# The seven products of a block step, in one fixed order

## The chip, the cores and the metric

The kernel runs on one core of one Trainium2 chip. The time is the device's own, in microseconds, from one execution of the whole program; a figure for a kernel is the median of several runs. The core has five engines that work side by side, each through its own list of instructions in order: TensorE (PE in the profile; its weight loads, which overlap the matmuls, are PEld), VectorE (DVE), ScalarE (ACT), GpSimd (POOL) and SyncE (SP), which here only starts transfers from the main memory. TensorE writes its sums to PSUM, a small memory of banks; ScalarE and VectorE read them there.

## The reference

Two layers of a diffusion backbone over 512 tokens of 1024 channels. The first mixes tokens by attention, the second by a Fourier transform; each ends in a gated feed-forward network (FFN) with a width-3 convolution over the tokens, between RMS norms that a conditioning vector scales and shifts:

```python
def conv_ffn(h, w_up, conv_w, conv_b, w_down):
    u = h @ w_up
    up = jnp.pad(u, ((0, 0), (1, 1), (0, 0)))
    u = up[:, :-2] * conv_w[0] + up[:, 1:-1] * conv_w[1] + up[:, 2:] * conv_w[2] + conv_b
    gate, val = jnp.split(u, 2, axis=-1)
    return (jax.nn.silu(gate) * val) @ w_down
```

Here `h` is 512 x 1024, `w_up` 1024 x 5632 and `w_down` 2816 x 1024. All is float32, and the result is the token stream after both layers.

## The kernel before

Everything is kept transposed: channels on the 128 partitions, tokens along the free axis. A float32 product is made of three matmuls on a rounded format (float32r): each operand is split into a high part, the rounded value, and a low part, what is left over, and `mm3` (lines 107 to 110) issues weight high x moving high (L108), weight high x moving low (L109) and weight low x moving high (L110) into the same PSUM tile. In the profile's rows the moving operand stands first, the weight second, so `mm<-hl,wh` is L109 and `mm<-hh,wl` is L110. `split` (L131) makes the parts: ScalarE casts the high one, VectorE subtracts to get the low one.

The hidden width of the FFN, 2816, is 22 steps of 128 columns; each makes one tile of the gate and one of the value (both 128 x 512), convolves them (L1412 on ScalarE, L1413 and L1415 on VectorE), gates them (L1425, L1426) and splits the result for the down product, which follows in groups of steps. Most steps, 10 in the first layer's FFN and 14 in the second's, are *block steps*. There the product of the two weight blocks (each 8 slices of 128 rows) with `h` is done as a 2 x 2 block product with seven block multiplications in place of eight: the weight is a 2 x 2 array (gate or value, first or second half of the channels), and so is `h` (halves of the channels, halves of the tokens). `seven_inputs` (L1296) forms the sums of blocks of `h` once for an FFN; products 1, 2 and 3 use blocks of `h` itself (`hh`, `hl` in the rows), products 4 to 7 the sums (`zh`, `zl`). `seven_weights` (L1310) forms the sums of weight blocks for each step, with three operations of VectorE (L1315, L1317, L1318), and splits them in four pieces: the weight of product 1; of 5 and 7; of 6 and 3; of 2 and 4. High and low parts of weights (`wh`, `wl`) go through five tiles each; the raw weights that arrive by DMA, and the sums, share three tiles (`raw`). A cast that finds no free weight tile waits until TensorE has read one for the last time.

`seven_products` (L1329) multiplies. Each product is 4 slices x 3 = 12 matmuls of 128 x 128 x 256. Two PSUM tiles of one bank each take them, x (which becomes the gate) and y (the value), each with a left and a right half of 256 columns:

| product | goes to | what reads it |
|---|---|---|
| 1 | right of y | copy L1349 into `xs`, left |
| 5 | right of x | copy L1351 into `ys`, right |
| 2 | left of x | |
| 6 | right of y, on top of 1 | copy L1354 into `xs`, right |
| 4 | left of y | |
| 3 | right of x, on top of 5 | add L1357: x + `xs` |
| 7 | right of y, on top of 6 | copy L1359 into `ys`, left; add L1360: y + `ys` |

The copies run on ScalarE, the adds on VectorE. TensorE may not write to a tile while a copy reads from it, whichever half either touches.

The list of each engine is not the order of the source. A planner orders all instructions before the program runs, by their place in the source, by what depends on what, and by its own estimate of times; an instruction that its estimate holds up is passed by one that is ready. `follow(i, j)` (L113) ties instruction i behind j on the same engine, without a semaphore. Before the change, it ties the first matmul of a product behind the last of the product that opened its tile (1 for y, 5 for x) and leaves the rest to the planner.

Of the kernel before, what the change touches and what calls it, by code (L numbers as in the profile page):

```python
# [85 lines left out]
def kernel(ctx: ExitStack, tc: tile.TileContext, a):  # L86
# [5 lines left out]
    def mk(pool, shape, dt=F32, tag=None, bufs=1):  # L92
        cnt[0] += 1
        n = nbufs.setdefault((id(pool), tag), (pool, bufs))[1]
        return pool.tile(shape, dt, tag=tag, name=f"{tag}_{cnt[0]}", bufs=n)
# [11 lines left out]
    def mm3(out, ah, al, bh, bl, start, stop, skip=False):  # L107
        i = PE.matmul(out, lhsT=ah, rhs=bh, start=start, stop=False, skip_group_check=skip)  # L108
        PE.matmul(out, lhsT=ah, rhs=bl, start=False, stop=False, skip_group_check=skip)  # L109
        return i, PE.matmul(out, lhsT=al, rhs=bh, start=False, stop=stop, skip_group_check=skip)  # L110


    def follow(i, j):  # L113
        tc.add_manual_dep(i.ins, j.ins.name, mybir.DependencyInfo(
            mybir.DependencyClass.NoSync, mybir.DependencyReason.DATA), reason="order")
# [553 lines left out]
    with ExitStack() as es:  # L669
# [27 lines left out]
        with ExitStack() as e1:  # L697
# [305 lines left out]
            for g, kind in enumerate(["kb", "vb", "qa"]):  # L1003
# [5 lines left out]
                for sh, sl, t0, kb in (blocks if kind[0] != "q" else blocks[:2]):  # L1009
                    ps = mk(pps, [P, 2, 256], F32, "mm", 6)  # L1010
# [26 lines left out]
        with ExitStack() as e2:  # L1037
# [86 lines left out]
            for head in range(8):  # L1124
# [6 lines left out]
                for j in range(TT):  # L1131
                    qs = slice(j * P, (j + 1) * P)
                    ps = S0.pop() if S0 else mk(aps, [P, 1024], F32, "S", 2)
# [176 lines left out]
    def seven_weights(l, fi):  # L1310
        r = raw([P, 2, KC, P], a["w_up"][l, fi])
        s = mk(wp, [P, 4, KH, P], F32, "raw", 3)
        a4 = r.rearrange("p i (c k) n -> p (i c) k n", c=2)

        for j in (V.tensor_tensor(out=s[:, 0:2], in0=a4[:, 3::-3], in1=a4[:, 2].unsqueeze(1).to_broadcast(  # L1315
                      [P, 2, KH, P]), op=ALU.add),
                  V.tensor_tensor(out=s[:, 2], in0=s[:, 0], in1=a4[:, 0], op=ALU.add),  # L1317
                  V.tensor_tensor(out=s[:, 3], in0=s[:, 2], in1=a4[:, 1], op=ALU.add)):  # L1318
            held(j)
        w = {}  # L1320
        for names, src in (("1", a4[:, 0:1]), ("57", s[:, 0:2]), ("63", s[:, 2:4]), ("24", a4[:, 1::2])):
            wh, wl = wpair([P, len(names), KH, P])
            split(wh, wl, src)
            for i, n in enumerate(names):
                w[n] = wh[:, i], wl[:, i]
        return w


    def seven_products(l, fi, pps, bs):  # L1329
        w = seven_weights(l, fi)  # L1330
        x, y = (mk(pps, [P, T], F32, "mm", 6) for _ in range(2))
        xs, ys = (mk(cp, [P, T], F32, "sq", 2) for _ in range(2))
        begun = {}


        def product(n, ps, h):
            (wh, wl), (bh, bl) = w[n], bs[n]
            new = id(ps) not in begun
            m = []
            for k in range(KH):  # L1340
                m += mm3(ps[:, halves[h]], wh[:, k, :], wl[:, k, :], bh[:, k, :], bl[:, k, :], new and k == 0,
                         k == KH - 1, True)
            if new:
                begun[id(ps)] = m[-1]
            else:
                follow(m[0], begun[id(ps)])

        product("1", y, 1)
        S.copy(out=xs[:, :HT], in_=y[:, HT:])  # L1349
        product("5", x, 1)  # L1350
        S.copy(out=ys[:, HT:], in_=x[:, HT:])  # L1351
        product("2", x, 0)
        product("6", y, 1)
        S.copy(out=xs[:, HT:], in_=y[:, HT:])  # L1354
        product("4", y, 0)
        product("3", x, 1)
        V.tensor_tensor(out=x, in0=x, in1=xs, op=ALU.add)  # L1357
        product("7", y, 1)
        S.copy(out=ys[:, :HT], in_=y[:, HT:])  # L1359
        V.tensor_tensor(out=y, in0=y, in1=ys, op=ALU.add)  # L1360
        return x, y
# [27 lines left out]
    def ffn(l, xp, ready, pre, mid, gem, plain=None):  # L1389
# [168 lines left out]
        for gi, (f0, nch) in enumerate(GROUPS[l]):  # L1558
            end = gi == len(GROUPS[l]) - 1
            for fi in range(max(f0, FIRST), f0 + nch):  # L1560
                if fi == SUMS[l]:
                    bs = seven_inputs(xp)
                if fi in SEVEN[l]:
                    cc = [conv(fi, i, u, None, i == 1) for i, u in enumerate(seven_products(l, fi, pps, bs))]
                else:
                    cc = []
                    for i, w in enumerate(up_weights(l, wpair, [fi])):
                        ps = mk(pps, [P, T], F32, "mm", 6)
                        m = [up_mm(ps, w, s) for s in halves]
                        follow(m[1][0][0], m[0][-1][1])  # L1570
                        cc.append(conv(fi, i, ps))
                gated(fi, cc[0], cc[1], f0)
                if l == 0 and fi not in SEVEN[l] and fi > FIRST + 4:
                    pump(gem, GP[0])
                if l:
                    pump(down, DOWN.get(fi, 0))
# [365 lines left out]
```

## Time and profile before

| | us |
|---|---|
| median of three runs | 1110.64 (1109.5 to 1110.91) |
| the profiled execution, its own time | 1112.16 |
| its span, first to last instruction | 1110.4 |
| PE busy | 1081.1 (97%) |
| VectorE busy | 894.8 (81%) |
| ScalarE busy | 595.2 (54%) |
| GpSimd busy | 128.5 (12%) |
| granted TensorE clock, mean | 0.996 of full |

The profile gives start and duration of each instruction, and for an engine's idle time what ended it. Matmuls overlap in the engine's pipeline: one lasts 0.28 us, but in an undisturbed run the next starts 0.11 us after it. So a TensorE that is shown busy may still be late, and the distance between starts is read instead. The 24 block steps lie between 357 and 607 us (first layer) and between 831 and 1055 us (second layer) of the span.

### The profile page before, as it was taken

What the parts mean: (1) busy time and instruction counts of PE and PEld (TensorE: products, weight loads), DVE (VectorE), ACT (ScalarE), POOL (GpSimd) and SP (SyncE); (2) the same over time, 40 slices, a digit from 0 to 9 for tenths busy, and PEclk for the clock granted to TensorE, in tenths of its full rate; (3) what the DMA queues carried; (4) which work ended last, traced back from release to release, by engine and by line L of the source; (5) the groups of instructions that cost most, each with busy time, mean ns of one, the idle gap of its engine ahead of it and who ended that gap; (6) DMA issues with size and microseconds to landing.
All of it is one profiled execution on the core that took longest, in us unless ns stands there. A gap on an engine that the chain in (4) does not pass through costs nothing.

```text
span 1110.4 us, 22277 instructions
## 1 busy us (share of the span) xinstructions
PE 1081.1 (97%) x9220; PEld 1011.4 (91%) x9220; DVE 894.8 (81%) x1459; ACT 595.2 (54%) x1048; POOL 128.5 (12%) x136
## 2 busy tenths in 40 slices
PE   9999999999999999999999998999999999999995
PEld 5699888869999999999999997989999999999995
DVE  5778877763689967878999788878997998979756
ACT  4442356665665633552556446668755654655543
POOL 0046123412100000000000133300000000000012
PEclk9999999999999999999999999999999999999998
DMA  9675100273231565227624600923205433332342
GB/s 368 273 256 209 39 7 33 76 275 143 77 153 43 181 233 213 106 86 272 236 77 175 231 22 21 279 82 143 86 29 198 145 107 118 105 103 88 106 148 77
DMA packets 33774, 156.01 MB, mean 140 GB/s; under 512 B 3460, under 2 KB 8196, under 8 KB 22024
## 3 DMA queue, kind: packets, MB, share of 16 engines
q1 hardware_dynamic: 32520, 150.39, 37.6%
q0 software_dynamic: 1152, 4.19, 1.5%
q8 instruction: 72, 1.18, 0.4%
q14 instruction: 30, 0.25, 0.1%
HBM read 148.28 MB, written 6.29 MB: 139 GB/s over the span
## 4 chain that ended last, share of the span: by engine, by line
PE 69%; DVE 18%; ACT 6%; DMA 4%; issue 2%; POOL 1%; SPq 0%; DVEq 0%; POOLq 0%; ACTq 0%
PE mm L108 20%; PE mm L109 18%; PE mm L110 18%; DVE wl L131 4%; ACT wh L131 2%; PE PT L1081 1%; DVE cv L1413 1%; DVE cv L1415 1%; DMA raw<-in_w_up 1%; DVE md_t L330 1%; DVE xT L332 1%; PE gm L108 1%; ACT yT L352 1%; PE O L109 1%; PE gm L110 1%
## 5 line engine op out<-in xcount | busy, mean ns | idle before, releaser
L131 ACT CAST wh<-raw 128x1024 fp32r<-128x1024 f32 (+2 forms) x207 | 190.7, 932 | 147.3 <-PE mm L109 96.9
L131 DVE TENSOR_TENSOR wl<-raw,wh 128x1024 fp32r<-128x1024 f32 (+2 forms) x205 | 219.4, 1076 | 59.3 <-ACT wh L131 56.7
L108 PE MATMUL mm<-hh,wh 128*128 128x256 f32 x856 | 240.2, 282 | 2.5 <-ACT sq L1351 1.8
L110 PE MATMUL mm<-hh,wl 128*128 128x256 f32 x856 | 236.9, 277 | 1.7 <-DVE wl L131 1.7
L109 PE MATMUL mm<-hl,wh 128*128 128x256 f32 x856 | 237.0, 277 | 0.4 <-DVE hl L355 0.3
L108 PEld LDWEIGHTS mm<-hh,wh 128*128 128x128 f32 x856 | 160.4, 188 | 8.5 <-ACT sq L1351 6.1
L110 PEld LDWEIGHTS mm<-hh,wl 128*128 128x128 f32 x856 | 160.9, 188 | 2.2 <-DVE wl L131 2.1
L109 PEld LDWEIGHTS mm<-hl,wh 128*128 128x128 f32 x856 | 160.8, 188 | 0.8 <-DVE hl L355 0.5
L108 PE MATMUL mm<-xh,wh 128*128 128x256 f32 x492 | 136.8, 279 | 0.0
L109 PE MATMUL mm<-xl,wh 128*128 128x256 f32 x492 | 136.6, 278 | 0.0
L110 PE MATMUL mm<-xh,wl 128*128 128x256 f32 x492 | 136.4, 277 | 0.0
L108 PE MATMUL mm<-zh,wh 128*128 128x256 f32 x384 | 109.4, 285 | 0.7 <-ACT sq L1354 0.5
L109 PE MATMUL mm<-zl,wh 128*128 128x256 f32 x384 | 106.3, 277 | 0.0
L110 PE MATMUL mm<-zh,wl 128*128 128x256 f32 x384 | 106.2, 277 | 0.0
L108 PEld LDWEIGHTS mm<-xh,wh 128*128 128x128 f32 x492 | 92.4, 188 | 1.2 <-issue 0.8
L109 PEld LDWEIGHTS mm<-xl,wh 128*128 128x128 f32 x492 | 92.4, 188 | 0.6 <-issue 0.4
L110 PEld LDWEIGHTS mm<-xh,wl 128*128 128x128 f32 x492 | 92.5, 188 | 0.1
L108 PEld LDWEIGHTS mm<-zh,wh 128*128 128x128 f32 x384 | 72.1, 188 | 6.0 <-ACT sq L1354 5.4
L110 PEld LDWEIGHTS mm<-zh,wl 128*128 128x128 f32 x384 | 72.2, 188 | 0.0
L109 PEld LDWEIGHTS mm<-zl,wh 128*128 128x128 f32 x384 | 72.1, 188 | 0.0
L305 POOL TENSOR_TENSOR gacc<-gacc,sq 128x256 f32<-128x256 f32 (+1 forms) x23 | 20.2, 880 | 396.8 <-ACT sq L303 396.4
L1412 ACT ACTIVATE cv<-mm,cols 128x512 f32<-128x512 f32 x59 | 45.8, 778 | 10.8 <-PE mm L110 6.1
(457 smaller groups left out, 2795.7 us busy)
## 6 DMA issues: line engine op xcount, KB each, us to landing
raw<-in_w_up SPq DMA_DIRECT2D x42, 1024.0 KB, 4.9
xT<-in_mod_r SPq DMA_DIRECT2D x20, 1024.0 KB, 5.0
raw<-in_w_down SPq DMA_DIRECT2D x32, 384.0 KB, 3.1
raw<-in_mod_p SPq DMA_DIRECT2D x8, 1024.0 KB, 5.0
raw<-in_w_down SPq DMA_DIRECT2D x16, 512.0 KB, 4.3
raw<-in_w_in SPq DMA_DIRECT2D x6, 1024.0 KB, 8.2
yT<-in_mod_r SPq DMA_DIRECT2D x10, 512.0 KB, 6.6
raw<-in_w_out SPq DMA_DIRECT2D x4, 1024.0 KB, 5.9
```

The source lines that it names most:

```text
L108: i = PE.matmul(out, lhsT=ah, rhs=bh, start=start, stop=False, skip_group_check=skip)
L109: PE.matmul(out, lhsT=ah, rhs=bl, start=False, stop=False, skip_group_check=skip)
L110: return i, PE.matmul(out, lhsT=al, rhs=bh, start=False, stop=stop, skip_group_check=skip)
L131: i = S.copy(out=h, in_=src), eng.tensor_tensor(out=l, in0=src, in1=f(h), op=ALU.subtract)
L305: G.tensor_tensor(out=self.acc[:, sl], in0=self.acc[:, sl], in1=sq[:, sl], op=ALU.add)
L330: m = V.scalar_tensor_tensor(out=t, in0=yT[:, k, hs], scalar=der[:, l, gi, k:k + 1], in1=R, op0=ALU.mult, op1=ALU.mult)
L332: return m, (eng or (G if k % 2 else V)).tensor_tensor(out=xT[:, k, hs], in0=xT[:, k, hs], in1=t, op=ALU.add)
L352: S.activation(out=yT[:, c, halves[h]], in_=yT[:, c, halves[h]], func=AF.Identity, bias=bm[:, c:c + 1], scale=am[:, c:c + 1])
L1081: PE.transpose(out=pt[:, j * P:(j + 1) * P], in_=Ps[j][:, off:off + P], identity=ident)
L1412: S.activation(out=cv, in_=ps, func=AF.Identity, bias=bc, scale=wc[1])
L1413: V.scalar_tensor_tensor(out=cv[:, 1:], in0=ps[:, :T - 1], scalar=wc[0], in1=cv[:, 1:], op0=ALU.mult, op1=ALU.add)
L1415: V.scalar_tensor_tensor(out=cv[:, :T - 1], in0=ps[:, 1:], scalar=wc[2], in1=cv[:, :T - 1], op0=ALU.mult, op1=ALU.add)
```

## The change

The products are issued in the order 1, 5, 6, 2, 3, 4, 7 instead of 1, 5, 2, 6, 4, 3, 7, and the first matmul of each is tied behind the last matmul of the product in front of it in that order, whichever tile it goes to. Copies and adds keep their places behind the products that they read. The first matmul that clears a tile's bank stays the first of 1 and of 5. Nothing else is different; the block steps of both FFNs go through this function.

```diff
         w = seven_weights(l, fi)
         x, y = (mk(pps, [P, T], F32, "mm", 6) for _ in range(2))
         xs, ys = (mk(cp, [P, T], F32, "sq", 2) for _ in range(2))
-        begun = {}
-
+        begun, last = {}, []
 
         def product(n, ps, h):
             (wh, wl), (bh, bl) = w[n], bs[n]
@@
             for k in range(KH):
                 m += mm3(ps[:, halves[h]], wh[:, k, :], wl[:, k, :], bh[:, k, :], bl[:, k, :], new and k == 0,
                          k == KH - 1, True)
-            if new:
-                begun[id(ps)] = m[-1]
-            else:
-                follow(m[0], begun[id(ps)])
+            begun[id(ps)] = True
+            if last:
+                follow(m[0], last.pop())
+            last.append(m[-1])
 
         product("1", y, 1)
         S.copy(out=xs[:, :HT], in_=y[:, HT:])
         product("5", x, 1)
         S.copy(out=ys[:, HT:], in_=x[:, HT:])
-        product("2", x, 0)
         product("6", y, 1)
         S.copy(out=xs[:, HT:], in_=y[:, HT:])
-        product("4", y, 0)
+        product("2", x, 0)
         product("3", x, 1)
         V.tensor_tensor(out=x, in0=x, in1=xs, op=ALU.add)
+        product("4", y, 0)
         product("7", y, 1)
         S.copy(out=ys[:, :HT], in_=y[:, HT:])
         V.tensor_tensor(out=y, in0=y, in1=ys, op=ALU.add)
```

## The prediction

> **What bounds the kernel now.** I read the page first, for the engine that is never free and for the chain that ended last.
>
> ```profile
> span 1110.4 us, 22277 instructions
> PE 1081.1 (97%) x9220; PEld 1011.4 (91%) x9220; DVE 894.8 (81%) x1459; ACT 595.2 (54%) x1048; POOL 128.5 (12%) x136
> ...
> PE 69%; DVE 18%; ACT 6%; DMA 4%; issue 2%; POOL 1%; SPq 0%; DVEq 0%; POOLq 0%; ACTq 0%
> ```
>
> TensorE carries the program, VectorE is next, and 69% of the last chain is matmuls. Second, I cut the 24 block steps out of the span: one window each, from the first matmul of product 1 to the first matmul behind product 7. The columns are length, then busy time and count of PE, PEld, DVE, ACT and POOL, then clock and DMA. Five of the 24 rows, and the sum over all:
>
> ```profile
> 356.83:367.60 10.77, 10.21 (x87) 9.82 (x85) 10.77 (x14) 6.76 (x11) 0.00 (x0) 1.00 0.30 99
> ...
> 543.19:553.45 10.26, 10.09 (x86) 9.70 (x85) 10.22 (x14) 7.05 (x12) 0.00 (x0) 1.00 0.53 194
> ...
> 596.56:606.93 10.37, 10.20 (x88) 9.80 (x86) 10.37 (x14) 6.85 (x11) 0.00 (x0) 1.00 0.58 206
> ...
> 886.93:898.41 11.48, 10.37 (x87) 9.78 (x85) 11.04 (x15) 6.33 (x10) 0.00 (x0) 1.00 0.37 127
> ...
> 1012.16:1022.27 10.11, 10.09 (x87) 9.70 (x85) 9.70 (x15) 5.65 (x10) 0.00 (x0) 1.00 0.44 148
> ...
> sum 247.61, PE 243.66 PEld 234.32 DVE 202.89 ACT 136.94 POOL 0.00; mean PE 10.15 PEld 9.76 DVE 8.45 ACT 5.71 POOL 0.00
> ```
>
> Every window holds 84 matmuls (7 products x 4 slices x 3), and PE looks busy in nearly all of it. The starts of single matmuls say something else. Here is PE in the window at 1012, around the two places that matter (start, duration, line, operands; zh marks products 4 to 7, hh products 1 to 3):
>
> ```profile
> 1014.77 0.28 PE L110 MATMUL mm<-zh,wl 128*128 128x256 f32 x1
> 1014.88 0.28 PE L108 MATMUL mm<-zh,wh 128*128 128x256 f32 x1
> ...
> 1015.22 0.28 PE L108 MATMUL mm<-zh,wh 128*128 128x256 f32 x1
> 1015.50 0.39 PE L108 MATMUL mm<-hh,wh 128*128 128x256 f32 x1
> 1015.73 0.28 PE L109 MATMUL mm<-hl,wh 128*128 128x256 f32 x1
> ...
> 1018.23 0.28 PE L108 MATMUL mm<-hh,wh 128*128 128x256 f32 x1
> 1018.52 0.39 PE L108 MATMUL mm<-zh,wh 128*128 128x256 f32 x1
> 1018.74 0.28 PE L109 MATMUL mm<-zl,wh 128*128 128x256 f32 x1
> ```
>
> Three matmuls take 1015.22 - 1014.88 = 0.34 us, 0.1133 from start to start; 0.28 is only the length of one in the pipeline. The order on PE is not the source's: product 5 (to 1014.77), four matmuls of 6, product 2 (1015.50), the other eight of 6, four of 3 (the last at 1018.23), product 4 (1018.52), the rest of 3, product 7. Ahead of 2 and ahead of 4 the spacing is 0.28 and then 0.23 instead of 0.11. The release rows name the cause:
>
> ```profile
> 1015.08 0.37 ACT L1351 COPY sq<-mm 128x256 f32<-128x256 f32 x1 [0.37 <-PE mm L110]
> ...
> 1018.09 0.37 ACT L1354 COPY sq<-mm 128x256 f32<-128x256 f32 x1 [1.07 <-PE mm L110]
> ```
>
> Call the copies behind products 1, 5 and 6 A, B and C (L1349, L1351, L1354). B ends at 1015.45 and product 2, which writes the other half of the tile B reads, starts at 1015.50; C ends at 1018.46 and product 4 starts at 1018.52. From the last matmul of a product to the first that may follow its copy pass 1015.50 - 1014.77 = 0.73 us, and only four matmuls (0.45 us) stand in between.
>
> **The change part by part.** Nothing is added or taken from the arithmetic: 84 matmuls, four copies and two adds a block stay. What changes is the order: 1, 5, 6, 2, 3, 4, 7, none cut open.
>
> *What is removed.* 24 x 84 = 2016 matmuls at 0.1133 are 228.4 us; the windows sum to 247.61, so 19.2 us are stall. The plain block at 1012 has 10.11 - 9.52 = 0.59, of which the two waits make (0.28 + 0.23 - 0.23) + (0.29 + 0.22 - 0.23) = 0.56. In the new order 12 matmuls (1.36 us) stand between 5 and 2, and 24 (2.72 us) between 6 and 4, against the 0.73 us needed: both waits go. With 12 in between the next start is due 13 x 0.1133 = 1.47 us after the last, with 24 it is 2.83, so a copy may be 0.74 and 2.1 us late before PE feels it.
>
> *What is late next.* Some stall stays.
>
> ```profile
> 891.87 0.38 PE L110 MATMUL mm<-hh,wl 128*128 128x256 f32 x1 [1.04 <-DVE wl L131]
> ...
> 567.72 0.28 PE L110 MATMUL mm<-zh,wl 128*128 128x256 f32 x1
> 567.93 0.38 PE L108 MATMUL mm<-zh,wh 128*128 128x256 f32 x1
> ...
> 547.48 0.39 PE L108 MATMUL mm<-hh,wh 128*128 128x256 f32 x1 [0.16 <-ACT sq L1351]
> ...
> 363.96 0.39 PE L108 MATMUL mm<-zh,wh 128*128 128x256 f32 x1 [0.55 <-ACT sq L1354]
> ```
>
> (a) In the block at 886.93 the third matmul of product 2 waits for its weight's low part. In the new order it is the block's 39th, due at 886.93 + 38 x 0.1133 = 891.24: 0.63 of wait and 0.11 of restart stay, and since VectorE is busy for 11.04 of 11.48 us there, what the block before gains may be waited away too: I keep 1.3. (b) A block right behind another (367.60, 543.19, 575.23) has copy B late: 2 is due at 543.19 + 36 x 0.1133 = 547.27 and may start at 547.48. 0.21 + 0.11, three times: 1.0. (c) Product 6 already stands right behind 5 and waits for copy A in four blocks, as at 567.93 (0.21 + 0.22 - 0.23 = 0.20): 0.8. (d) The block at 356.83 has C late; 4 is due at 356.83 + 60 x 0.1133 = 363.63, starts at 363.96: 0.4 with restart. (e) Slower spacing in some blocks, and starts behind matmuls of other stages: 1.2, the remainder of the sum over the windows. 19.2 - 4.7 = 14.5.
>
> *What is moved on other queues.* C comes 12 matmuls (1.36 us) earlier on ScalarE, and so does the add that closes tile x on VectorE. Weight tiles come free at other places: that of 6 and 3 after 60 matmuls instead of 72, that of 4 and 2 after 72 instead of 64. The first cast that waits for a free tile, as here, thus waits for the 60th instead of the 64th matmul, 0.45 us earlier, the second is where it was:
>
> ```profile
> 1005.90 2.01 ACT L131 CAST wh<-raw 128x1024 fp32r<-128x1024 f32 x2 [1.61 <-PE mm L109]
> ```
>
> No DMA and no POOL work is moved (POOL is 0.00 in every window). The bond is between instructions of one engine, so it adds no semaphore; behind a waiting product stands all of PE, and other products can no longer be drawn ahead of it. Bounds of that: below, nothing; above, the 1.32 us gap of 891.87 (from 890.55) in each block, 24 x 1.21 = 29 us. I take 0 beyond (a) to (d): the product that would be drawn ahead stood behind the same copies.
>
> *What VectorE gives back.* Nine of the 24 windows have VectorE busy for 9.7 us or more (356.83 is the first, 1012.16 the last); in those quoted at 356.83, 543.19 and 596.56 it has less than 0.1 us free. Work can slide out of such a block, since next to most of them stand plain steps; the bounds are nothing lost and all that these nine blocks would gain, 5.3 us (14.5 less the 9.2 of the rival below). I take 2.1, nearer to the lower end because VectorE is busy for only 202.89 of 247.61 over all blocks.
>
> Sum: 14.5 - 2.1 = 12.4 us. Against the profiled execution's own 1112.16 us that is 1099.8 (1.8 of it lie outside the span of 1110.4, and nothing here touches them); that execution lies 1.5 above the median of the runs, 1110.64, so for a median I forecast **1098.2**.
>
> The windows' PE busy sum, 243.66 of 247.61, would leave only 3.95 us to win, and 1106.7. The Trainium skill (Perfetto Trace Analysis, Identifying the Most-Contended Engine) says that matmul busy time is a bad measure of TensorE's headroom, since matmuls are pipelined, and prefers the weight loads' busy share; by that, 247.61 - 234.32 = 13.3 us are open. The starts agree with the skill's side: a 0.28 us matmul covers a wait of 0.28 us without showing it.
>
> **Rivals.**
>
> *VectorE sets the pace where it is full.* For it: the full windows, and 18% of the chain on VectorE. Against it: its casts wait for PE (1.61 at 1005.90), not the other way. Then the nine blocks with 9.7 us or more (lengths over 9.52 sum to 8.15) give nothing; of the other 15 blocks' 11.05, (c) and most of (e), 1.8, stay as well: 9.2 won, 1101.4, and a little worse if neighbours suffer.
>
> *Only the idle time that PE shows can be won*, 3.95 us: 1106.7. Against it: the starts.
>
> *The gain is given back.* Each place ahead of the end that waits for a weight, a landing or VectorE keeps its date, as 891.87 does: 1110. For it: VectorE, ScalarE and DMA hold 28% of the chain. Against it: almost all of these wait for PE earlier on, and move with it.
>
> *Slower: the copies fall behind casts.* ScalarE works in order, and here copy B stood behind a cast and a convolution step:
>
> ```profile
> 545.42 1.07 ACT L131 CAST wh<-raw 128x1024 fp32r<-128x1024 f32 x1
> 546.37 0.80 ACT L1412 ACTIVATE cv<-mm,cols,ncw 128x512 f32<-128x512 f32 x1
> 547.04 0.39 ACT L1351 COPY sq<-mm 128x256 f32<-128x256 f32 x1
> ```
>
> If the new plan puts both ahead of A and of B in every block, each copy is up to 1.07 + 0.80 = 1.87 late, less 0.74 of cover, plus 0.11: 1.24, and PE has nothing else to do. Twice in 24 blocks is 59.5, against 17.2 won (19.2 less 2.0): 1153. It decides from about 0.36 us a copy beyond the cover; for one copy in each block it is 29.8 - 17.2: 1123. Against it: in the block at 1012 the copies start as soon as their product ends. The Trainium skill (PSUM — Partial Sum Buffer, Engine vs sequencer instructions) states that ScalarE's queue is strictly first in, first out; the rows above agree, and it speaks for this rival.
>
> That the change does nothing would need the planner to keep the cut order; the bond forbids it within a block, so it gets no share.
>
> **How the numbers follow.** Forecast 0.70; VectorE 0.13; shown idle time only 0.05; given back 0.06; slower 0.06. What a measurement can tell from no change is 0.2%, 2.2 us: faster 0.70 + 0.13 + 0.05 = 0.88, same 0.06, slower 0.06. The range: at its low end nothing is lost but (c) and (e), 17.2 us won: 1093.5; at its high end stands the VectorE case with neighbours that lose 3.6 more, 5.6 won: 1105.
>
> **What would show it.** Right: per block one unbroken run of 1, 5, 6, 2, 3, 4, 7 with 0.11 spacing; PE waiting for L1351 and L1354 next to never; windows that sum to about 235; the block at 886.93 still waiting for a wl. VectorE's case: new PE waits on wl L131 in the nine full blocks. Slower: PE waits on L1349 or L1351 of more than 0.3 us. I am wrong if the windows shrink and the span does not, or if copies drift.

## The result and the profile after

The kernel after took 1098.22 us in the median of four runs (1097.91 to 1102.09), the kernel before 1110.07 us (1109.07 to 1110.91) in the runs beside it. The ratio is 0.9891, with a 95% interval of 0.9869 to 0.9912: about 12 us faster. One execution in all the runs below, of the kernel cut after six, took 1179.04 us at a granted clock of 0.847 and is left out of that kernel's figures (with it its median is 1110.28, the 1110.3 of an expectation below). The profiled execution of after took 1097.91 us, 14.25 less than the profiled one of before (1112.16).

The page of the kernel after, with the same lines as before:

```profile
span 1096.1 us, 22277 instructions
...
PE 1069.7 (98%) x9220; PEld 1007.4 (92%) x9220; DVE 896.3 (82%) x1459; ACT 594.2 (54%) x1048; POOL 127.8 (12%) x136
...
PE 71%; DVE 15%; ACT 5%; DMA 4%; issue 3%; POOL 1%; SPq 0%; DVEq 0%; POOLq 0%; ACTq 0%
```

The instructions are the same in number, and the work of VectorE, ScalarE and GpSimd is unchanged within 1.5 us. What is shorter is the span, and TensorE's busy time with it (1081.1 to 1069.7 us). The 24 block steps of after, each from the first matmul of product 1 to the first behind product 7 (columns as before):

```profile
356.95:366.85 9.90, 9.90 (x87) 9.90 (x85) 9.88 (x14) 6.34 (x10) 0.00 (x0) 1.00 0.29 108
366.85:376.91 10.06, 9.92 (x87) 9.72 (x85) 10.06 (x12) 7.00 (x12) 0.00 (x0) 1.00 0.60 182
...
538.86:549.05 10.19, 9.75 (x87) 8.94 (x85) 10.19 (x14) 6.78 (x13) 0.00 (x0) 1.00 0.66 247
...
880.41:891.24 10.83, 9.94 (x86) 9.72 (x85) 10.83 (x16) 6.45 (x11) 0.00 (x0) 1.00 0.40 135
...
999.71:1009.23 9.52, 9.52 (x86) 9.52 (x85) 9.14 (x13) 5.34 (x9) 0.00 (x0) 1.00 0.45 154
...
sum 233.87, PE 231.84 PEld 229.73 DVE 207.39 ACT 137.41 POOL 0.00; mean PE 9.66 PEld 9.57 DVE 8.64 ACT 5.73 POOL 0.00
```

The sum fell from 247.61 to 233.87 us: 13.74 of the 14.25 us lie inside the 24 blocks. Fourteen of them take 9.52 or 9.53 us, which is 84 times 0.1133, so nothing at all is lost there. The block at 999.71 is one. Its matmuls around the places where product 2 and product 4 begin (start, duration, line, operands):

```profile
1002.32 0.28 PE L110 MATMUL mm<-zh,wl 128*128 128x256 f32 x1
1002.43 0.28 PE L108 MATMUL mm<-zh,wh 128*128 128x256 f32 x1
...
1003.68 0.28 PE L110 MATMUL mm<-zh,wl 128*128 128x256 f32 x1
1003.79 0.28 PE L108 MATMUL mm<-hh,wh 128*128 128x256 f32 x1
...
1006.40 0.28 PE L110 MATMUL mm<-hh,wl 128*128 128x256 f32 x1
1006.51 0.28 PE L108 MATMUL mm<-zh,wh 128*128 128x256 f32 x1
```

Product 5 ends with 1002.32, all twelve matmuls of 6 follow, and 2 starts at 1003.79, 0.11 us behind the last of them; 4 starts at 1006.51, 0.11 behind the last of 3. Who waited for the copies says the same over all 24 blocks. Copy B, first in the kernel before (L1351), then after (L1350); the columns are total us and times:

```profile
L1351 ACT COPY sq<-mm x24: 365/373/395, 359.8 to 1047.6; 128x256 f32<-128x256 f32 x24
...
  PEld mm L108: 6.1, 20
  PE mm L108: 1.8, 7
```

The same view of the kernel after:

```profile
L1350 ACT COPY sq<-mm x24: 365/373/393, 360.0 to 1034.0; 128x256 f32<-128x256 f32 x24
...
  PEld mm L108: 1.1, 1
  PE mm L108: 0.9, 1
```

TensorE's weight loads waited for copy B 20 times before and once after. Copy C before (L1354):

```profile
L1354 ACT COPY sq<-mm x24: 368/373/376, 363.5 to 1050.6; 128x256 f32<-128x256 f32 x24
...
  PEld mm L108: 5.4, 24
  PE mm L108: 0.5, 1
```

And after (L1352), where the list of those who waited is empty:

```profile
L1352 ACT COPY sq<-mm x24: 363/372/374, 361.4 to 1035.3; 128x256 f32<-128x256 f32 x24
...
who waited for it (us, times):
busy tenths in 40 slices 0000000000000000000000000000000000000000
```

For copy C 24 loads waited before and none waits after.

Ten blocks are over 9.53 us. The three longest waits that PE's own rows show in them:

```profile
543.48 0.38 PE L110 MATMUL mm<-hh,wl 128*128 128x256 f32 x1 [0.42 <-DVE wl L131]
...
574.27 0.39 PE L110 MATMUL mm<-hh,wl 128*128 128x256 f32 x1 [0.35 <-DVE wl L131]
...
885.68 0.39 PE L108 MATMUL mm<-hh,wh 128*128 128x256 f32 x1 [0.89 <-ACT sq L1350]
```

And ScalarE's rows ahead of the last of these:

```profile
884.74 0.62 ACT L131 CAST wh<-raw 128x512 fp32r<-128x512 f32 x1 [1.68 <-DMA raw<-in_w_up]
885.26 0.36 ACT L1350 COPY sq<-mm 128x256 f32<-128x256 f32 x1
```

The block at 880.41 waits for copy B, which stands on ScalarE behind a cast, and that cast waited 1.68 us for a transfer to land. Product 5, which B copies, was long done, and so was product 6 behind it (its last matmul starts at 884.51).

### The profile page after: what moved, and what is told of

It reads as the page before. It is cut to its first block, busy times and chain, and to the rows that moved or that the text cites. A ratio compares the mean times of both kernels' runs of the same rounds, so it can differ in the third digit from the quotient of the medians.

```text
span 1096.1 us, 22277 instructions
## 1 busy us (share of the span) xinstructions
PE 1069.7 (98%) x9220; PEld 1007.4 (92%) x9220; DVE 896.3 (82%) x1459; ACT 594.2 (54%) x1048; POOL 127.8 (12%) x136
## 4 chain that ended last, share of the span: by engine, by line
PE 71%; DVE 15%; ACT 5%; DMA 4%; issue 3%; POOL 1%; SPq 0%; DVEq 0%; POOLq 0%; ACTq 0%
PE mm L108 20%; PE mm L109 19%; PE mm L110 19%; DVE wl L131 3%; PE PT L1081 1%; ACT wh L131 1%; DVE cv L1412 1%; DVE md_t L330 1%; DMA raw<-in_w_up 1%; DMA xT<-in_xT 1%; DMA xl<-in_mod_r 1%; DVE cv L1414 1%; DVE xT L332 1%; PE gm L108 1%; ACT yT L352 1%
## 5 line engine op out<-in xcount | busy, mean ns | idle before, releaser
L131 DVE TENSOR_TENSOR wl<-raw,wh 128x1024 fp32r<-128x1024 f32 (+2 forms) x205 | 219.7, 1078 | 26.0 <-ACT wh L131 25.9
L108 PE MATMUL mm<-zh,wh 128*128 128x256 f32 x384 | 106.8, 278 | 0.3 <-ACT sq L1348 0.2
```

Of the source, the lines that this page charges most:

```text
L131: i = S.copy(out=h, in_=src), eng.tensor_tensor(out=l, in0=src, in1=f(h), op=ALU.subtract)
```

## The experiments

Two sums over TensorE's starts are used below. They cover both FFNs, some 4035 matmuls. *Late starts*: every start more than 0.165 us behind the one ahead, counted with what it exceeds 0.1134. *Wide spacing*: starts 0.115 to 0.130 behind the one ahead, counted in the same way. The second was not foreseen: undisturbed matmuls came either every 113.4 ns or every 117.8 ns (the expectations call the first fast, the second slow).

| kernel | order in a block | span | late starts | wide spacing | span less both |
|---|---|---|---|---|---|
| before | 2 behind four matmuls of 6 | 1110.4 | 21.3 | 1.9 | 1087.2 |
| after | 1, 5, 6, 2, 3, 4, 7 | 1096.1 | 7.6 | 1.6 | 1086.9 |
| after_again | the same program | 1097.8 | 6.6 | 3.8 | 1087.4 |
| e2_chain_only | 1, 5, 2, 6, 4, 3, 7 | 1114.5 | 25.9 | 1.7 | 1086.9 |
| e3_two_behind_six | 1, 5, 6, 2, 4, 3, 7 | 1104.0 | 12.3 | 5.1 | 1086.6 |
| e8_cover3 | 6 and 3 cut after 3 matmuls | 1111.8 | 24.7 | 1.3 | 1085.8 |
| cover5 | cut after 5 | 1108.2 | 19.6 | 1.4 | 1087.2 |
| e7_cover6 | cut after 6 | 1107.1 | 9.3 | 7.9 | 1089.9 |
| cover6_again | the same program | 1108.8 | 10.1 | 9.1 | 1089.6 |
| cover7 | cut after 7 | 1100.6 | 9.6 | 6.4 | 1084.6 |
| e9_cover9 | cut after 9 | 1103.6 | 7.8 | 6.8 | 1089.0 |
| e4_copies_first | as after, copies given precedence | 1094.4 | 9.2 | 0.3 | 1084.9 |
| after_less_vector | as after, less VectorE work | 1102.1 | 12.0 | 4.4 | 1085.7 |
| before_less_vector | as before, less VectorE work | 1114.0 | 23.1 | 3.1 | 1087.8 |

The spans differ by 20 us, the last column by 5 (1084.6 to 1089.9, mean 1087.1). So these two sums carry most of what the fourteen profiles differ by.

### The order alone, and the bond alone

The kernel before with only the new source order, and its old bonds, compiles into the same list of instructions on each of the five engines as the kernel after. The bond of each product to the one in front therefore does nothing in this change; the order does it all. The bond with the old order:

```diff
         product("5", x, 1)
         S.copy(out=ys[:, HT:], in_=x[:, HT:])
+        product("2", x, 0)
         product("6", y, 1)
         S.copy(out=xs[:, HT:], in_=y[:, HT:])
-        product("2", x, 0)
+        product("4", y, 0)
         product("3", x, 1)
         V.tensor_tensor(out=x, in0=x, in1=xs, op=ALU.add)
-        product("4", y, 0)
```

(This and the diffs below are against the kernel after, unless another is named.)

> The products keep the old source order 1, 5, 2, 6, 4, 3, 7, and each is bound whole behind the one in front, so nothing stands between product 5 and product 2 or between 6 and 4. My theory (the matmuls that stand between a product and the one that follows its copy decide, 0.73 us are needed): each of the two waits costs 0.73 - 0.11 + 0.11 = 0.73 us, 1.46 a block, 35 us in 24 blocks on top of 1098: about 1133, slower than before. Rival, VectorE sets the pace in the nine full blocks and hides it there: 15 blocks pay, about 1120. Rival, the binding itself brings the gain: about 1098.

Measured: 1118.23 us, ratio 1.0068 [1.0046, 1.0091]: slower than before, but by some 7 us and not 22. PE at one block:

```profile
940.82 0.28 PE L110 MATMUL mm<-zh,wl 128*128 128x256 f32 x1
940.94 0.28 PE L108 MATMUL mm<-xh,wh 128*128 128x256 f32 x1
...
941.28 0.28 PE L109 MATMUL mm<-hl,wh 128*128 128x256 f32 x1
941.62 0.38 PE L108 MATMUL mm<-hh,wh 128*128 128x256 f32 x1
```

Behind product 5 (last start 940.82) the planner drew four matmuls of other steps (the first two read xh and xl, the next two hh and hl) ahead of product 2, which starts at 941.62, 0.34 behind them. So the copies are covered by four matmuls, as in the kernel before, and the same wait stays. The bond keeps other products of the block out, not other steps; my 1133 had forgotten these. What its profile has over that of before is another wait: starts that wait for a weight's high or low part make 6.1 us of its late starts, against 1.2 before. The planner stops at four, 0.45 us, where the trace shows 0.73 needed.

### How much must stand between

The kernel after with products 6 and 3 cut, so that only a part of them stands ahead of 2 and of 4. For three matmuls:

```diff
-        def product(n, ps, h):
+        def product(n, ps, h, ks=range(KH)):
...
-            for k in range(KH):
+            for k in ks:
...
+        ca, cb = range(1), range(1, KH)
...
-        product("6", y, 1)
-        S.copy(out=xs[:, HT:], in_=y[:, HT:])
+        product("6", y, 1, ca)
         product("2", x, 0)
-        product("3", x, 1)
-        V.tensor_tensor(out=x, in0=x, in1=xs, op=ALU.add)
+        product("6", y, 1, cb)
+        S.copy(out=xs[:, HT:], in_=y[:, HT:])
+        product("3", x, 1, ca)
         product("4", y, 0)
+        product("3", x, 1, cb)
+        V.tensor_tensor(out=x, in0=x, in1=xs, op=ALU.add)
```

> The new order, but product 6 is cut after its first slice and 2 stands behind it, and 3 is cut after its first slice and 4 stands behind it; all bound. Three matmuls of cover instead of twelve. My theory: the next start is due 4 x 0.1133 = 0.45 us after the last one, 0.73 are needed, 0.28 + 0.11 = 0.39 a wait, 48 waits, 18.7 us on top of 1098: about 1117, slower than before by 7 (before has four matmuls of cover). Rival, the gain came from another plan for ScalarE and VectorE and not from the cover: no relation, 1098 to 1110.

Measured: 1116.79 us, ratio 1.0051 [1.0028, 1.0074], as expected, with 24.7 us of late starts against 21.3. With `range(2)`, six matmuls:

> As with three matmuls of cover, but cut after the second slice: six matmuls of cover. My theory: the next start is due 7 x 0.1133 = 0.79 us after the last, 0.73 are needed, so no wait as long as the copy starts on time, and 0.06 us to spare; copies that are late by 0.2 to 0.4 us in some blocks cost 2 to 4 us in all: 1100 to 1102. If twelve matmuls are needed for the whole gain (late copies are the rule): 1104 or more.

Measured: 1109.55 us, ratio 0.9992 [0.9974, 1.001]. The waits went as they should (9.3 us of late starts), and the gain did not come: 1784 matmuls were spaced 117.8 ns, 7.9 us in all. With `range(3)`, nine matmuls:

> As with six matmuls of cover, but 6 and 3 are cut after the third slice: nine matmuls of cover. With six, the waits were gone (9.3 us of late starts in both FFNs, 7.6 in the changed kernel) and yet the time was 1110: 1784 of the matmuls followed each other by 0.118 instead of 0.1134 us, 7.9 us in sum. Theory S (a start that is late by 0.05 us leaves TensorE in the slower spacing until the next disturbance): with nine the copies are 0.4 us early, the marginal starts go, and the spacing is 0.1134 again: 1098 to 1101. Rival (products that are cut open, tiles that alternate more often, cause the slower spacing): about 1108 as with six.

Measured: 1104.28 us, ratio 0.9931 [0.9904, 0.9959]; late starts 7.8, wide spacing 6.8. That lies between the two expectations. Here the wide spacing lies mainly in two long stretches, cut products and whole ones alike. One of them as a window (length, then busy time and count by engine, clock, DMA):

```profile
770.77:887.37 116.60, 116.60 (x992) 116.60 (x991) 106.52 (x149) 69.61 (x103) 0.00 (x0) 1.00 0.35 119
```

And a window of about as many matmuls of the kernel after:

```profile
954.93:1066.92 111.99, 111.99 (x990) 111.99 (x989) 90.56 (x122) 59.37 (x94) 4.81 (x6) 1.00 0.35 120
```

990 spaces in 116.60 us are 117.8 ns, 988 in 111.99 are 113.4 ns. The granted clock is 1.00 in both, so it is not the clock; and since the products outside the blocks are not cut, it is not the cutting by itself.

### The same program twice

> The changed kernel once more, beside the others of this call: 1097 to 1102. Theory S expects its slower matmuls in the same places as in its first profile, up to a few blocks; a spacing that is drawn by chance at each execution would show elsewhere, and times that spread over 4 us or more.

Measured: 1099.73 us, ratio 0.99 [0.9875, 0.9924]. Its late starts are 6.6 us against 7.6, its wide spacing 3.8 against 1.6. The block that takes 9.52 us at 824.53 in the first profile takes 9.89 in this one, with TensorE never idle and full clock:

```profile
825.85:835.74 9.89, 9.89 (x86) 9.89 (x85) 6.75 (x11) 5.37 (x10) 0.00 (x0) 1.00 0.53 180
```

So the spacing is not fixed by the program alone: of 348 starts that are wide in the first profile 344 are wide again, and some 510 more have come. And the kernel cut after six, once more:

> The program of e7_cover6 once more, unchanged, for one profile. There 1784 matmuls of the two FFNs came every 117.8 ns in place of 113.4 ns, 7.9 us in all, in stretches from one restart to the next. If the spacing is drawn anew at restarts, in each execution: the number of slowly spaced matmuls differs by several hundred, and the same stretch of the program is fast in one profile and slow in the other. If it belongs to the program (its operands, their places, its own order): the same stretches are slow again, 7 to 9 us in all.

Measured: 1110.53 us in its one run; 2052 matmuls at the wide spacing, 9.1 us. Matched one by one over the FFNs, some 1320 matmuls are wide in both profiles, 470 only in the first, 740 only in the second. Both expectations hold in part: much of it comes back at the same places, the rest does not. One of those places is where product 4 starts in a block of the first layer. PE's rows in the first of the two profiles:

```profile
439.07 0.28 PE L110 MATMUL mm<-hh,wl 128*128 128x256 f32 x1
439.18 0.33 PE L108 MATMUL mm<-zh,wh 128*128 128x256 f32 x1
439.35 0.28 PE L109 MATMUL mm<-zl,wh 128*128 128x256 f32 x1
```

The window behind it, to the next disturbance:

```profile
439.35:457.48 18.13, 18.13 (x155) 18.13 (x155) 15.87 (x21) 10.79 (x16) 0.00 (x0) 1.00 0.45 173
```

Copy C of this block on ScalarE:

```profile
438.70 0.37 ACT L1355 COPY sq<-mm 128x256 f32<-128x256 f32 x1 [2.68 <-PE mm L110]
```

The copy ends just in time, at 439.07: the first matmul of product 4 starts 0.11 behind that and 0.11 behind the last of 3, but the second comes 0.17 behind the first, 0.05 late. The window shows the next 154 spaces, 18.13 us or 117.7 ns each. In the second execution the same thing happens at the same place (438.25, then 438.42), and the 154 spaces behind it take 18.14 us.

Over all fourteen profiles I sorted each single disturbance that came upon the close spacing by its length. Where one start came 0.1645 to 0.1705 us behind the one ahead, the wide spacing followed in 31 of 31; 29 of these lie in the two executions cut after six. These bounds were drawn after the starts had been sorted: where one start without a second late one behind it came 0.150 to 0.1645 behind, the wide spacing followed in 0 of 8. Where it came 0.1705 to 0.1765 behind, the wide spacing followed in 2 of 21 (20 of these have a second late start, some 0.22, behind them, and lie in cover5), behind 0.190 to 0.250 in 16 of 108, and behind 0.279 to 0.300, the usual wait of the kernel before, in 2 of 88. A disturbance of 0.250 to 0.279 that came upon the wide spacing ended it in 21 of 22. This suggested a test: one matmul more or less in the cut must take the 0.05 us lateness away.

### One matmul less, one more

The kernel cut after six, with the cut at any single matmul (7 for cover7, 5 for cover5):

```diff
-        def product(n, ps, h, ks=range(KH)):
+        def product(n, ps, h, part=range(3 * KH)):
...
-            for k in ks:
-                m += mm3(ps[:, halves[h]], wh[:, k, :], wl[:, k, :], bh[:, k, :], bl[:, k, :], new and k == 0,
-                         k == KH - 1, True)
+            for q in part:
+                k, t = divmod(q, 3)
+                i = PE.matmul(ps[:, halves[h]], lhsT=(wl if t == 2 else wh)[:, k, :], rhs=(bl if t == 1 else bh)[:, k, :],
+                              start=new and q == 0, stop=q == 3 * KH - 1, skip_group_check=True)
+                m.append(i)
...
-        ca, cb = range(2), range(2, KH)
+        ca, cb = range(7), range(7, 3 * KH)
```

> Products 6 and 3 are cut after their fifth matmul, so five matmuls (0.57 us) cover the copies of products 5 and 6 in place of six (0.68 us) in e7_cover6; they need 0.73 us. Theory N (a matmul that starts just late, about 0.05 us behind its time, is followed by the spacing of 117.8 ns; one that is 0.17 us late by that of 113.4 ns): here most starts in question are about 0.16 us late, so the waits are longer than in e7_cover6 (about 16 us against 9 to 10 in both FFNs) and the spacing is fast again (under 4 us of it, against 8 to 9): 1104 to 1107 us, faster than e7_cover6 (1110.3) although it waits longer. Rival (cutting products 6 and 3 slows the spacing, or the spacing is drawn at random at each restart): 8 us of slow spacing remain and the waits grow: 1114 to 1117. Rival (only the waits count): 1106 plus what e7_cover6 lost for its own reason, so between 1110 and 1116.

Measured: 1109.91 us, ratio 1.0001 [0.999, 1.0011]. The spacing did what theory N says: 1.4 us of the wide one instead of 7.9 and 9.1, though the products are cut as before. The waits came out larger than I had worked out, 19.6 us and not 16, so the time is that of the kernel cut after six and 3 us above the expected range. By the time alone the rival that only waits count (1110 to 1116) does better; it is the count of wide spaces that speaks for theory N. PE at the same place as above:

```profile
438.37 0.28 PE L1341 MATMUL mm<-hl,wh 128*128 128x256 f32 x1
438.55 0.39 PE L1341 MATMUL mm<-zh,wh 128*128 128x256 f32 x1
438.77 0.28 PE L1341 MATMUL mm<-zl,wh 128*128 128x256 f32 x1
```

The window behind it:

```profile
438.77:455.78 17.01, 17.01 (x151) 17.01 (x151) 14.86 (x20) 9.84 (x15) 0.00 (x0) 1.00 0.46 178
```

Now the start is 0.18 behind and the next 0.22: a real wait, longer than the one with six, and the 150 spaces behind it take 17.01 us, 113.4 ns each.

> Products 6 and 3 are cut after their seventh matmul, one matmul later than in e7_cover6: 0.79 us cover the copies that need 0.73 us, so nearly no start of this kind is late, not even by 0.05 us. Theory N: without the starts that are just late the slow spacing has nothing that brings it on 20 times and more: at most 5 us of it against 8 to 9 in e7_cover6, late starts 7 to 8 us, time 1098 to 1103 us, 8 us or more faster than e7_cover6 by one matmul's place. Rival (cutting the products slows the spacing): 1108 to 1110. Rival (the spacing is drawn at random, once drawn it stays until the next disturbance): anything from 1098 to 1110, with stretches of several hundred matmuls at one spacing.

Measured: 1103.22 us, ratio 0.9943 [0.9927, 0.9958]: by the ratios 5 to 6 us below the kernel cut after six, for one matmul's place, just above the expected range and less than the 8 us expected. Late starts are 9.6 us and wide spacing is 6.4, more than the 5 expected. It no longer comes from many short stretches: one of 605 spaces begins at 815.46, ahead of the second layer's blocks, behind a wait of another kind. That is what the rival of a drawn spacing looks for. So theory N holds for what brings the wide spacing on 11 and 18 times with six matmuls; beside it the spacing is also set, one way or the other, at long waits (13 of 45 disturbances of 0.4 to 0.9 us that came upon the close spacing were followed by the wide one), and stays. The starts show a sign of which it will be. Of the late starts upon the close spacing that have a second late one behind them, the wide spacing followed in 16 of 16 where the second came 0.226 or 0.227 behind the first, and in 7 of 220 where it came 0.220 to 0.224 behind. This was seen in the traces afterwards and not tested; what in the engine decides it stays open.

### Only product 2 moved

```diff
-        product("6", y, 1)
+        m6 = product("6", y, 1)
         S.copy(out=xs[:, HT:], in_=y[:, HT:])
-        product("2", x, 0)
+        follow(product("2", x, 0)[0], m6[-1])
+        product("4", y, 0)
         product("3", x, 1)
         V.tensor_tensor(out=x, in0=x, in1=xs, op=ALU.add)
-        product("4", y, 0)
```

(with the bonds of the kernel before for the rest)

> Only product 6 is put in front of 2 and 2 bound whole behind it; 4, 3 and 7 stay in the old source order and with the old bonds. The planner then issues 1, 5, 6, 2, 4, 3, 7, nothing cut: twelve matmuls between 5 and 2 and twelve between 6 and 4. My theory: twelve are as good as 24, so the whole gain, 1098. Rival, copy C needs the longer cover because ScalarE starts it late: half the gain, about 1104.

Measured: 1103.1 us, ratio 0.9938 [0.9916, 0.9959]. Twelve matmuls now stand ahead of 4 as well as ahead of 2. The whole gain, as I had expected it from twelve, did not come; the time is that of the rival, 1104. Of its 12.3 us of late starts three waits on copy C make 2.7, and 5.1 us are wide spacing; the 24 matmuls ahead of 4 in the kernel after are worth up to 5 us more, though part of that is spacing, which differs between executions.

### Is it VectorE, or the copies?

The third tap of the convolution is left out in the block steps, in the kernel after and in the kernel before:

```diff
-            V.scalar_tensor_tensor(out=cv[:, :T - 1], in0=ps[:, 1:], scalar=wc[2], in1=cv[:, :T - 1],
-                                   op0=ALU.mult, op1=ALU.add)
+            if fi not in SEVEN[l]:
+                V.scalar_tensor_tensor(out=cv[:, :T - 1], in0=ps[:, 1:], scalar=wc[2], in1=cv[:, :T - 1],
+                                       op0=ALU.mult, op1=ALU.add)
```

> The changed kernel, but in the block steps the convolution leaves out its third tap, one VectorE operation of 0.74 us a tile: 48 operations, 35 us of VectorE's work. If VectorE holds back only what the full blocks show (waits on wl, 1.2 us, and starts near them), the time falls by 1 to 3 us: 1095 to 1097. If it sets the pace over the FFNs, by 5 or more: below 1093. If it holds nothing: 1098.

Measured: 1104.44 us, ratio 0.994 [0.9916, 0.9963], slower than after by some 5 us although VectorE is busy for 29 us less. The waits for a weight's low part fell from 1.19 us of late starts to 0.24, but the copies are waited for again. Copy A makes 3.7 us of late starts in place of 0.9, copy B 3.0 in place of 1.3. The view of copy A:

```profile
L1348 ACT COPY sq<-mm x24: 359/366/389, 358.7 to 1039.4; 128x256 f32<-128x256 f32 x24
...
  PEld mm L108: 3.7, 9
```

And of copy B:

```profile
L1350 ACT COPY sq<-mm x24: 358/372/389, 360.0 to 1039.6; 128x256 f32<-128x256 f32 x24
...
  PEld mm L108: 3.1, 3
```

> The kernel before, with the third tap of the convolution left out in the block steps (48 VectorE operations of 0.73 us, about 35 us of VectorE's work; the output lacks that tap). It is the pair of after_less_vector, which was slower than the kernel after (1104.4 us against 1098 to 1100). If VectorE's work sets a part of the time before: faster than the kernel before by 2 us or more, so 1108 or less beside 1110 to 1112. If the waits on copies B and C set it, as I now hold: the 44 waits of about 0.22 us stay, and the time is 1109 to 1113. If leaving VectorE work out disturbs the order of ScalarE's work as it did in after_less_vector: 1114 to 1117.

Measured: 1113.4 us, ratio 1.0031 [1.0013, 1.005], slower here too, between the second and the third expectation. Neither kernel gains from a lighter VectorE. The edit is not clean, as the planner orders ScalarE's work anew and copies come late by that; a small gain that VectorE hides could be covered by it. Last, the kernel after with its three copies given precedence over all other work on ScalarE:

```diff
-        S.copy(out=ys[:, HT:], in_=x[:, HT:])
+        with later(-10000):
+            S.copy(out=ys[:, HT:], in_=x[:, HT:])
```

(the same for copies A and C)

> The changed kernel, but the copies behind 1, 5 and 6 are given a higher place in the planner's queue, ahead of casts that are ready at the same time. In the changed kernel 2.1 us of late starts still wait for these copies. If they can be had by order alone: 1096. If the casts that are put off make weights late, or the planner has them in that order already: 1098 or more.

Measured: 1098.32 us, ratio 0.9883 [0.9857, 0.991], beside 1099.73 for the kernel after on the same chip: no difference that can be told. Its late starts are even 9.2 us, some 4.6 of them by copies A and B against 2.2 in the kernel after. ScalarE at the worst place:

```profile
868.82 0.62 ACT L131 CAST wh<-raw 128x512 fp32r<-128x512 f32 x1 [2.59 <-DMA raw<-in_w_up]
869.35 0.36 ACT L1352 COPY sq<-mm 128x256 f32<-128x256 f32 x1
```

And PE behind it:

```profile
869.76 0.39 PE L108 MATMUL mm<-hh,wh 128*128 128x256 f32 x1 [1.35 <-ACT sq L1352]
```

Precedence doesn't help here: the cast that waits for its transfer was still planned ahead of copy B. This is the block in front of the one that waits longest in the kernel after (885.68). That one still waits too, behind a cast that waits 1.74 us for its landing:

```profile
884.33 0.39 PE L108 MATMUL mm<-hh,wh 128*128 128x256 f32 x1 [0.69 <-ACT sq L1352]
```

So the longest waits on copy B that are left are set by landings.

## Why the prediction was right, and where not

The forecast was 1098.2 us, the median came to 1098.22. By its own steps:

*What bounds the kernel, and the two waits.* Right, and shown. The two waits a block were hidden in a PE that looked busy; they went (20 and 24 waiting loads became 1 and 0), and the time fell with them. PE's idle time, 3.95 us in the windows before, was no measure of it: 13.74 us were won in them. The Trainium skill (Perfetto Trace Analysis, Identifying the Most-Contended Engine) prefers the weight loads' busy share to the matmuls'; the 13.3 us that were open by that are close to the 13.74. The match is partly chance: after still has 4.1 us without a weight load (233.87 - 229.73), so 9.2 of the 13.3 went, and the rest came out of the loads' own busy time (234.32 to 229.73). The rival built on PE's idle time, 1106.7, is out, and so are "given back" and "slower" as results.

*The sum.* It took 12.4 us off the profiled execution; 14.25 came off. In the windows 19.2 us of stall became 233.87 - 228.4 = 5.5, where 6.8 were to stay. The medians differ by 11.85 only: the first profiled execution of before lay 1.5 us above the median of its first runs, that of after 0.3 below its own, and the median of before came out 0.6 lower in the runs beside after. The exact hit is thus partly luck. By the profiled executions the sum was 1.9 us too small; by the medians it was 0.55 too large, and the 0.57 by which the median of before came out lower cancels that. Single executions of one program spread by 3 to 5 us, once by 9, part of which is the spacing.

*(a) The block at 886.93: 1.3 to stay.* The size was right (10.83 - 9.52 = 1.31), the cause wrong. I had the third matmul of product 2 waiting for its weight's low part. What waits is the first one, for copy B behind a cast that waits for a landing. That is the mechanism of the rival "slower", in one block of 24 (and by 0.08 us in the block in front of it, at 870.77). There the 1.36 us of cover were not enough.

*(b) Late copies in blocks that stand behind another, 1.0, and VectorE's give-back, 2.1.* Oversized together, and the mechanism of (b) was wrong. The blocks at 366.85, 538.86 and 570.36 exceed 9.52 us by 0.54, 0.67 and 0.64, 1.85 in all, but no start in them waits for copy B. In two of them PE waits for a low part from VectorE (0.42 and 0.35 us), as the VectorE rival had it, but not in nine. The nine blocks with VectorE full before, which were to give nothing by that rival, went from 8.15 us over 9.52 to 3.54: 4.6 us were won in them. The forecast had 5.3 for them less 2.1, so 0.7 and not 2.1 was given back. In the runs with less work for VectorE nothing was won.

*(c) Waits of product 6 for copy A, 0.8.* Right in size: 0.94 us of late starts by copy A in after. *(d) Copy C late in the first block, 0.4.* That wait is gone. The block still has 0.38 over, all of it wide spacing. *(e) Spacing, 1.2.* 1.6 us over both FFNs, in the first profile; I took it for a constant of the blocks, and it differs between executions (3.8 in the next).

*The bond.* I wrote that the bond forbids the planner to cut the products. It isn't needed: the order alone gives the same program. And where it is kept without the order, other steps' matmuls go in between and the time rises.

## What to carry to other kernels

Read the distance between starts, not the busy share, to find what TensorE waits for: a wait as long as one pipelined matmul doesn't show as idle. Where a product overwrites what a copy still reads, count how long the hand-over takes in the trace (here 0.73 us, against the four matmuls of 0.45 us that the planner had put there) and order the work so that clearly more than that stands in between; six matmuls, 0.05 us too few, were no better here than five or four, while seven were 5 to 6 us better. When a change is smaller than some 5 us in a kernel like this, look at the spacing of undisturbed matmuls in several executions before giving it a cause.

## What had not been expected of the hardware

The same matmuls (128x256, weights of 128x128, granted clock 1.00) run at two spacings, 113.4 and 117.8 ns, for stretches of up to 990, and change between them nearly always at a disturbance. (Once, at 914.07 in the kernel cut after nine, the wide spacing began with no start more than 0.120 behind the one ahead.) A start 0.165 to 0.170 us behind the one ahead was followed by the wider one in 31 of 31 cases, nearly all in one program; single late starts a little shorter never were (0 of 8), and of those a little longer, mostly with a second late start behind them, 2 of 21 were. The stretches behind these starts make some 5 of the 7.9 us in the first execution cut after six and some 7 of the 9.1 in the second; the starts themselves cost under 1 us. So a kernel can lose several times what such starts cost, and a longer wait can be cheaper than a short one: five matmuls of cover took as long as six (1109.91 and 1109.55 us), with twice the late starts. That the wider spacing follows these starts was tested with five and seven matmuls; why it does, and why the second start behind a long wait tells which spacing follows, stays open.
